# Expert stage of a two-block transformer: the down product of one expert moved behind gate and up of the next

## The chip, the cores and the metric

One core of a Trainium2 chip runs the whole program in one launch. The metric is device time in microseconds (us); lower is better. TensorE does the matmuls, VectorE, ScalarE and GpSimd the elementwise work, SyncE issues the weight loads.

## The reference, cut to what matters

Two transformer blocks over 256 tokens of width 1024. The first block and the attention of the second are dense and are not touched here. The last stage is a mixture of 32 experts, four for each token, followed by a residual sum and a layer norm:

```python
h = xb @ w_gu[e] + b_gu[e]                      # [tokens, 2048], w_gu[e] is [1024, 2048]
h_gate, h_up = jnp.split(h, 2, axis=-1)
h_gate = jnp.minimum(h_gate, 7.0)
h_up = jnp.clip(h_up, -7.0, 7.0)
act = h_gate * jax.nn.sigmoid(1.702 * h_gate) * (h_up + 1.0)
y = act @ w_down[e] + b_down[e]                 # w_down[e] is [1024, 1024]
# out = layer_norm(alpha * h + sum over a token's four experts of gate * y)
```

All weights are float32: 8 MB and 4 MB for each expert, 403 MB (384 units of 1 MB) for the stage.

## The kernel before, in words

Dense layers come first and end in `land` (residual sum, router, each token's slot in its experts). `moe_body` then goes through the 32 experts in turn, each with 64 token slots.

**Weights.** A unit is 1 MB, [128, 2048] float32. An expert has 8 units of `w_gu` (one for each 128 rows, `gate_up`) and 4 of `w_dn` (`down`). `expert_units` sets their order. `fetch` puts each into the next of 21 buffers in turn (pools early, more, xt, merge, ring, parts, moe), by SyncE's queue; a buffer is loaded again when the matmuls that read its old unit are done. `prefetch` fills buffers during the dense layers.

**Half-array work.** With 64 tokens a matmul of `gate_up` (L1260) or `down` (L1292) takes 64 of the array's 128 columns. Two of them, for the two output halves, stand next to each other and run at the same time. A float32 matmul is two instructions, so a unit is 8.

**Whole-array work.** `turn_act` (4 transposes of the activation, L1278), the bias (2 matmuls in `gated_unit`, L1266), `gather` (picks the tokens of two experts by one-hot matmuls, 32 instructions, L1150), `back` (gated one-hots turned, L1204), and `combine` (adds an expert's result into four PSUM sums, 64 rows by 128 columns, 8 instructions, L1375). One-hots and gates of two experts (EG = 2) are made together.

**Order.** For expert e: units 2 to 7 of gate and up; `combine(e - 1)` after the first of these; the bias, then the activation (`gated_unit`, on VectorE and ScalarE); the start of expert e + 1 (its gather, when a new pair begins) and its first unit; `turn_act` of e; the second unit of e + 1 (LEAD = 2); then `down` of e. The scheduler of the language places TensorE's instructions by its own priorities within the dependences, except in the last expert, where the written order holds. The residual is added in two lumps at experts 16 and 31.

```python
u = self.gated_unit(*bank[e])
if e % EG == 0:
    weights(e)
start(e + 1)
product(e + 1, 0)
aT = self.turn_act(u)
for k in range(1, LEAD):
    product(e + 1, k)
y = self.down(aT, lambda i: self.unit_of_expert())
```

`scratch` has 7 buffers for activations, one-hots, results and pick rows; `ps_tr` and `ps_mm` have two PSUM banks each. `rest` is a loop over blocks of tokens beyond an expert's 64 slots.

Of the kernel before, what the change touches and what calls it, by code (L numbers as in the profile page):

```python
# [31 lines left out]
LEAD = 2  # L32
# [20 lines left out]
class Net:  # L53
# [109 lines left out]
    def half_product(self, ps, xT, w, half, js=range(4)):  # L163
        """ps += chunks js of a half of xT times a [4 k, 512] weight unit."""
# [45 lines left out]
    def parts_of(self, ps, hi, lo, gain):  # L210
        """psum chunks [P, n, m] (times gain[:, chunk]) as two float32r parts."""
# [11 lines left out]
    def transposed(self, src, hi, lo, gain=None):  # L223
        """src [P, D] -> its transposed chunks in hi, lo [P, KD, P]."""
# [11 lines left out]
    def begin(self, gu):  # L236
        """The first group's weights and both tiles of x, in BEGIN's order."""
# [29 lines left out]
    def enter(self, t, gain):  # L267
        """x of tile t, turned, with the norm's gain; and its 1 / rms (None without a norm)."""
# [8 lines left out]
    def ffn_body(self, ins, gu, dn, then, hooks):  # L277
        """What enters next: its first tile, and what finishes the second, for when the next first product is out."""
# [75 lines left out]
    def head_norm(self, raw, heads, dh, eps=1e-6, pool=False):  # L354
        """raw [P, heads, dh] normalised over dh in place."""
# [10 lines left out]
    def turn_heads(self, raw, n, outs):  # L366
        """raw [P, n * 128] -> n transposes; outs: (first, count, dest [P, count, P], scale)."""
# [7 lines left out]
    def scores(self, qT, kT, nk, dh):  # L375
        """4 heads' scores [P, 2, 256] x 2: head 2p+s at [s][:, p]."""
# [11 lines left out]
    def softmax(self, sc, nk, bias, scale=True):  # L388
        """exp(score + bias - max) [P, 4, nk], over its row sums unless not scale, and the sums [P, 4]."""
# [27 lines left out]
    def turn_blocks(self, blocks, dest, vector):  # L417
        """Transposes of [P, P] blocks (up to 4) into dest [P, n, P]."""
# [12 lines left out]
    def turn_causal(self, e, t, heads, pT):  # L431
        """e [P, heads, nk] of token tile t into pT [P keys, heads, 3, P]: (tile, key block) 00, 10, 11."""
# [3 lines left out]
    def weigh(self, pT, v, dh, o_hi, o_lo):  # L436
        """Heads' outputs over both token tiles, turned: [P, chunks, T] in two parts; v(h, b): [P, dh]."""
# [23 lines left out]
    def mem_kv(self, l):  # L461
        """Keys (turned) and values of the memory, for layer l."""
# [14 lines left out]
    def rope(self, raw, t):  # L477
        """raw [P, 8, 64]: 4 heads of q, 4 of k -> rotated with the gains."""
# [511 lines left out]
    def route(self, t, ps, less, r):  # L990
        """Which experts tile t's tokens go to, and their slots there (less AWAY); a step a turn."""
# [33 lines left out]
    def gate(self, t):  # L1025
        """Tile t's gates [P, NE], 0 where an expert is not chosen."""
# [13 lines left out]
    def plan_rest(self):  # L1040
        """Blocks of SLOTS tokens beyond an expert's first: how many [1, 1], first and end block per expert."""
# [24 lines left out]
    def rest(self, n, first, end, pick, spare, acc, ln):  # L1066
        """Adds to acc what tokens past an expert's first SLOTS get, one block a turn, by way of two spare tiles,
        and makes the output anew."""
# [3 lines left out]
        with self.tc.For_i(0, n, 1):  # L1072
# [38 lines left out]
            banks = self.gate_up_banks(pk)  # L1111
            for k in range(KD):
                self.gate_up(banks[0], xg[:, k], load(k, gu[0, k * P:(k + 1) * P]), k)
            y = self.down(self.turn_act(self.gated_unit(*banks)),
                          lambda i: load(i, dn[0, i * 256:(i + 1) * 256].rearrange("(c p) d -> p c d", c=2)))
            for h in range(2):
                hs = slice(64 * h, 64 * h + 64)
                for t in range(NT):
# [3 lines left out]
                    nc.tensor.matmul(acc[t][h], gT[t][hs, 0], y[hs], start=False, stop=True)  # L1122
# [21 lines left out]
    def gather_banks(self):  # L1144
        """Where the first gather goes, a bank for two chunks."""
# [6 lines left out]
    def gathered(self, k2, ps, xg):  # L1152
        """Two chunks of what was gathered, with the norm's gain and bias."""
# [9 lines left out]
    def gather(self, hot, xg):  # L1163
        """xg [P, KD, n] = the chosen tokens' columns of x."""
# [8 lines left out]
    def one_hot(self, t, es):  # L1173
        """Tile t's one-hots [P, experts * SLOTS] of the slots of some experts."""
# [11 lines left out]
    def gated(self, hot, gate, n):  # L1186
        """One-hots times gates, twice over: [P, n, 2, SLOTS] per tile."""
# [9 lines left out]
    def back(self, gated, n):  # L1197
        """Gated one-hots turned: per tile [P = (copy, slot), n, P tokens]."""
        nc = self.nc
        out = []  # L1200
        for t in range(NT):
            ps = self.t(self.ps_tr, [P, 4, P], F32, "tr")
            for e in range(n):
                nc.tensor.transpose(ps[:, e], gated[t][:, e].rearrange("p c s -> p (c s)"), self.ident)  # L1204
            gT = self.t(self.moep, [P, n, P], F32, f"back{t}") if n > 1 else self.scr(P).unsqueeze(1)
            nc.scalar.activation(gT, ps[:, :n], AF.Copy, scale=1.0 / 1.702)
            out.append(gT)
        return out

    def expert_units(self):  # L1210
        """The experts' weights in the order of their use: LEAD units of the next one's go before an expert's w_dn."""
        a = self.a
        gu = lambda e, ks: (a["w_gu"][e, k * P:(k + 1) * P] for k in ks)
        yield from gu(0, range(LEAD))
        for e in range(NE):
            yield from gu(e, range(LEAD, KD))
            if e + 1 < NE:
                yield from gu(e + 1, range(LEAD))
            for i in range(4):
                yield a["w_dn"][e, i * 256:(i + 1) * 256].rearrange("(c p) d -> p c d", c=2)  # L1220

    def fetch(self, src=None):
        """The next tile of the rings in turn, with src in it (the last unit in halves)."""
# [15 lines left out]
    def prefetch(self, name, n=None):  # L1239
        """A ring of its own for the experts' first units, loaded ahead (n of them)."""  # L1240
# [7 lines left out]
    def gate_up_banks(self, pick):  # L1248
        nc = self.nc
        ps = [self.t(self.ps_mm, [P, 512], F32, "mm") for _ in range(2)]  # L1250
        pk = self.t(self.scratch, [P, 512], F32R, "s")[:, :2 * SLOTS].rearrange("p (h s) -> p h s", h=2)
        nc.gpsimd.tensor_copy(pk, pick.unsqueeze(2).to_broadcast([P, 2, SLOTS]))
        return ps, pk.rearrange("p h s -> p (h s)")

    def gate_up(self, ps, xk, w, k):
        """ps: the gate's and the up's bank [(half, slot), 512] += x's chunk k . w."""
        for gu in range(2):
            for h in range(2):
                c = gu * D + h * 512
                self.nc.tensor.matmul(ps[gu][64 * h:64 * h + 64], xk, w[:, c:c + 512], start=k == 0, stop=False)  # L1260

    def gated_unit(self, ps, pk):
        """The expert's bias and activation, times 1.702: [(half, slot), 512]."""
        nc = self.nc
        for gu in range(2):
            nc.tensor.matmul(ps[gu], pk, self.brow[:, gu], start=False, stop=True)  # L1266
# [16 lines left out]
    def down(self, aT, unit):  # L1283
        """y [(half, slot), 512]; unit(i): the weights."""
# [18 lines left out]
    def down_bias(self, acc):  # L1303
        """The experts' output biases, times the gates."""
# [12 lines left out]
    def moe_body(self):  # L1317
        nc, a = self.nc, self.a
        hot, banks = self.land()
        acc = [[None, None], [None, None]]  # L1320
        group, bank, back = {}, {}, {}

        def start(e):
            bank[e] = self.gate_up_banks(self.pick[:, e])
            if e % EG == 0:
                es = slice(e, e + EG)
                xg = self.t(self.moep, [P, KD, EG * SLOTS], F32, "xg")
                group[e // EG] = xg, [self.one_hot(t, es) for t in range(NT)] if e else hot
                if e:
                    self.gather(group[e // EG][1], xg)  # L1330

        def product(e, k):
            xg, hot = group[e // EG]
            if e == 0 and k % 2 == 0:
                for j in range(2):
                    for t in range(0 if k >= GATHERED else 1, NT):
                        self.gather_tile(t, k + j, hot[t], banks[k // 2][:, j], t == j == 0, t == j == 1)
                self.gathered(k // 2, banks[k // 2], xg)
            j = e % EG
            self.gate_up(bank[e][0], xg[:, k, j * SLOTS:(j + 1) * SLOTS], self.unit_of_expert(), k)  # L1340

        def weights(e):
            if e == 0:
                for t in range(NT):
                    self.gate(t)
# [209 lines left out]
```

## Time and profile before

| what | value |
|---|---|
| three timed runs | 2157.06, 2160.55, 2159.61 us; median 2159.61 |
| span of the profiled execution | 2158.0 us (no other time is shown for it) |
| TensorE busy (matmul) | 2053.7 us, 95% |
| VectorE, ScalarE, GpSimd busy | 885.3, 691.3, 116.7 us |
| SyncE's weight queue | 596.68 MB |
| mean granted clock of TensorE | 0.988 |

The span runs from the first to the last instruction. Busy time of TensorE is modelled from instructions that overlap in its pipeline, so how much work it does is better read from the distance between starts. The expert stage fills the time from about 1150 us to the end.

### The profile page before, as it was taken

The numbers are of one execution on the slowest core, as the hardware profiler recorded it, in microseconds if no ns is written. First come the engines' busy times: TensorE is split into PE (matmuls) and PEld (weight loads), VectorE is DVE, ScalarE is ACT, GpSimd is POOL, SyncE is SP. The second block draws the span as 40 slices with busy tenths as digits, with TensorE's granted clock in tenths as the row PEclk, the third lists the DMA queues.
The fourth block names the chain that finished last, engine by engine and source line by source line (L and its number), as shares of the span: only waits on it lengthen the run. The fifth ranks groups of instructions, "written<-read, shape, count | busy, mean of one in ns | idle before, by whom it ended". The sixth has DMA issues, their size and how long they took to land.

```text
span 2158.0 us, 24764 instructions
## 1 busy us (share of the span) xinstructions
PE 2053.7 (95%) x9375; PEld 1254.2 (58%) x9375; DVE 885.3 (41%) x2128; ACT 691.3 (32%) x1542; POOL 116.7 (5%) x180
## 2 busy tenths in 40 slices
PE   8999999999999879999999999999999999999996
PEld 7888778888888767888885333333333333333332
DVE  7554876557765887554543110111011011111113
ACT  7454665446553556543541000000000000000000
POOL 0000320000000340000100000000000000000000
PEclk9999999999999999999999999999999999999998
DMA  8463446554554334644569999999999999999980
GB/s 313 175 224 142 144 146 215 190 197 182 193 185 156 139 117 182 228 177 165 202 223 382 364 420 421 421 420 420 417 412 373 389 409 409 420 406 411 408 338 21
DMA packets 101996, 601.98 MB, mean 279 GB/s; under 512 B 10065, under 2 KB 10113, under 8 KB 46193
## 3 DMA queue, kind: packets, MB, share of 16 engines
q1 hardware_dynamic: 100496, 596.68, 70.7%
q0 software_dynamic: 1232, 3.65, 0.5%
q8 instruction: 75, 1.23, 0.2%
q14 instruction: 49, 0.39, 0.0%
q10 hardware_dynamic: 144, 0.03, 0.0%
HBM read 599.27 MB, written 1.05 MB: 278 GB/s over the span
## 4 chain that ended last, share of the span: by engine, by line
PE 89%; DVE 7%; issue 2%; POOL 1%; ACT 1%; DMA 1%; SPq 0%; DVEq 0%; ACTq 0%; POOLq 0%
PE mm L1260 23%; PE tr L1292 10%; PE mm L159 10%; PE mm L160 10%; PE mm L161 10%; PE acc L159 4%; PE acc L1375 4%; PE acc L160 4%; PE acc L161 4%; PE tr L1150 3%; DVE s L1268 1%; PE tr L294 1%; DVE s L1296 1%; PE tr L1278 1%; DVE lo L144 1%
## 5 line engine op out<-in xcount | busy, mean ns | idle before, releaser
L144 DVE TENSOR_TENSOR lo<-w,hi 128x512 fp32r<-128x512 f32 x706 | 455.8, 696 | 189.8 <-ACT hi L142 188.2
L142 ACT ACTIVATE hi<-w 128x512 fp32r<-128x512 f32 x720 | 398.1, 626 | 219.0 <-PE mm L161 92.3
L159 PE MATMUL mm<-hi,w 128*128 128x512 f32 x960 | 383.8, 400 | 3.1 <-ACT w L251 2.7
L160 PE MATMUL mm<-lo,w 128*128 128x512 f32 x960 | 377.5, 394 | 0.6 <-DVE lo L144 0.6
L161 PE MATMUL mm<-hi,w 128*128 128x512 f32 x960 | 376.9, 393 | 0.0
L1260 PE MATMUL mm<-w,xg 128*64 128x512 f32 x1480 | 369.9, 600 | 7.0 <-DVE s L1268 7.0
L1269 ACT ACTIVATE s<-s 128x512 f32<-128x512 f32 x32 | 20.1, 629 | 742.4 <-DVE s L1268 720.7
L1260 PEld LDWEIGHTS mm<-w,xg 128*64 128x64 f32 x1480 | 103.4, 137 | 210.5 <-issue 171.9
L159 PEld LDWEIGHTS mm<-hi,w 128*128 128x128 f32 x960 | 181.7, 189 | 41.7 <-ACT w L251 3.1
L160 PEld LDWEIGHTS mm<-lo,w 128*128 128x128 f32 x960 | 182.0, 190 | 38.0 <-DVE lo L144 2.3
L161 PEld LDWEIGHTS mm<-hi,w 128*128 128x128 f32 x960 | 181.7, 189 | 38.5 <-DVE w L220 0.2
L1268 DVE TENSOR_SCALAR s<-mm 128x512 f32<-128x512 f32 x32 | 22.1, 692 | 413.6 <-PE mm L1266 413.4
L1292 PE MATMUL tr<-w,s 128*64 128x512 f32 x728 | 162.8, 592 | 0.7 <-ACT s L1280 0.7
L1296 DVE COPY s<-tr 128x512 f32<-128x512 f32 x32 | 22.1, 691 | 343.3 <-PE tr L1292 343.3
L159 PE MATMUL acc<-hi,ah 128*128 128x512 f32 x336 | 131.7, 392 | 0.0
L160 PE MATMUL acc<-lo,ah 128*128 128x512 f32 x336 | 130.9, 390 | 0.0
L161 PE MATMUL acc<-hi,al 128*128 128x512 f32 x336 | 130.9, 390 | 0.0
L1375 PE MATMUL acc<-s,back 64*128 64x512 f32 x256 | 92.6, 626 | 22.3 <-DVE s L1296 22.3
L1292 PEld LDWEIGHTS tr<-w,s 128*64 128x64 f32 x728 | 52.6, 137 | 104.1 <-issue 97.4
L1150 PE MATMUL tr<-s,x 128*128 128x128 f32 x496 | 69.5, 289 | 22.1 <-DVE s L1181 21.6
L287 ACT ACTIVATE s<-mm,rs 128x256 f32<-128x256 f32 x88 | 41.7, 474 | 148.2 <-PE mm L161 144.7
L1150 PEld LDWEIGHTS tr<-s,x 128*128 128x128 f32 x496 | 60.8, 196 | 44.5 <-issue 26.7
(328 smaller groups left out, 1976.0 us busy)
## 6 DMA issues: line engine op xcount, KB each, us to landing
w<-w_gu SPq DMA_DIRECT2D x185, 1024.0 KB, 9.7
w<-w_dn SPq DMA_DIRECT2D x90, 1024.0 KB, 9.9
w<-gu SPq DMA_DIRECT2D x86, 1024.0 KB, 4.8
w<-dn SPq DMA_DIRECT2D x44, 1024.0 KB, 4.8
lo<-w_gu SPq DMA_DIRECT2D x36, 1024.0 KB, 10.0
hi<-w_gu SPq DMA_DIRECT2D x35, 1024.0 KB, 9.6
w<-w_in SPq DMA_DIRECT2D x32, 1024.0 KB, 4.8
hi<-w_dn SPq DMA_DIRECT2D x19, 1024.0 KB, 9.5
```

The source lines that it names most:

```text
L142: self.nc.scalar.activation(hi[:, s], raw[:, s], AF.Copy)
L144: engine.tensor_tensor(lo[:, s], raw[:, s], hi[:, s].bitcast(F32), op=ALU.subtract)
L159: mm(out, lh, rh, start=start, stop=False)
L160: mm(out, lh, rl, start=False, stop=False)
L161: mm(out, ll, rh, start=False, stop=stop)
L287: nc.scalar.activation(si, ps[:, :FG], AF.Silu, scale=rs)
L1150: self.nc.tensor.matmul(out, self.x[t][:, k * P:(k + 1) * P], hot, start=start, stop=stop)
L1260: self.nc.tensor.matmul(ps[gu][64 * h:64 * h + 64], xk, w[:, c:c + 512], start=k == 0, stop=False)
L1268: nc.vector.tensor_scalar_min(g, ps[0], 7.0)
L1292: nc.tensor.matmul(py[64 * d:64 * d + 64], aT[:, j, 64 * h:64 * h + 64], w[:, c * D + d * 512:c * D + d * 512 + 512], start=i == 0 and c = ...
L1296: nc.vector.tensor_copy(y, py)
L1375: nc.tensor.matmul(acc[t][h], gT[t][hs, e % EG], y[hs], start=e == 0, stop=e == NE - 1)
```

## The change

TensorE's order is now the written one for the whole stage. A block per expert, `between(e)`, holds all whole-array work: the activation of e - 1 turned, the bias of e (now first in its sums, so it opens the accumulation), the gather of a new pair, `combine(e - 2)`, the turned gates. Then follows one stretch of half-array work: the 8 units of gate and up of e, and the 4 units of down of e - 1. The weights are fetched in that order. One-hots, gated one-hots and pick rows are made one block ahead, on VectorE and GpSimd (`ahead`). The residual comes in pieces in blocks 8 to 13, the output biases in block 3 (before: expert 1). The last norm's rows are fetched before the last four units. `back` turns the gates of both token tiles into one PSUM bank with one copy. The activation of e is computed while down of e - 1 runs.

```diff
-        yield from gu(0, range(LEAD))
-        for e in range(NE):
-            yield from gu(e, range(LEAD, KD))
-            if e + 1 < NE:
-                yield from gu(e + 1, range(LEAD))
-            for i in range(4):
-                yield a["w_dn"][e, i * 256:(i + 1) * 256].rearrange("(c p) d -> p c d", c=2)
+        for e in range(NE + 1):
+            if e < NE:
+                yield from (a["w_gu"][e, k * P:(k + 1) * P] for k in range(KD))
+            if e:
+                yield from (a["w_dn"][e - 1, i * 256:(i + 1) * 256].rearrange("(c p) d -> p c d", c=2)
+                            for i in range(4))
...
+    def gate_up_banks(self, pk):
+
         ps = [self.t(self.ps_mm, [P, 512], F32, "mm") for _ in range(2)]
+        for gu in range(2):
+            self.nc.tensor.matmul(ps[gu], pk, self.brow[:, gu], start=True, stop=False)
+        return ps
...
+        ps = self.t(self.ps_tr, [P, 4, P], F32, "tr")
         for t in range(NT):
-            ps = self.t(self.ps_tr, [P, 4, P], F32, "tr")
             for e in range(n):
-                nc.tensor.transpose(ps[:, e], gated[t][:, e].rearrange("p c s -> p (c s)"), self.ident)
...
+                nc.tensor.transpose(ps[:, t * n + e], gated[t][:, e].rearrange("p c s -> p (c s)"), self.ident)
...
+    def picker(self, pick):
+
+        pk = self.t(self.scratch, [P, 512], F32R, "s")[:, :2 * SLOTS].rearrange("p (h s) -> p h s", h=2)
+        self.nc.gpsimd.tensor_copy(pk, pick.unsqueeze(2).to_broadcast([P, 2, SLOTS]))
+        return pk.rearrange("p h s -> p (h s)")
...
+        def first_gather(k2):
+            for j in range(2):
+                k = 2 * k2 + j
+                for t in range(0 if k >= GATHERED else 1, NT):
+                    self.gather_tile(t, k, hots[0][t], banks[k2][:, j], t == j == 0, t == j == 1)
+            self.gathered(k2, banks[k2], xg[0])
...
+        sums = {8 + 3 * t: residual(t) for t in range(NT)}
+
+        def between(e):
+
+            g = e // EG
+            if e:
+                aT = self.turn_act(u.pop(e - 1))
+            if e < NE:
+                u[e] = self.gate_up_banks(pk.pop(e))
+                if e % EG == 0:
+                    xg[g] = self.t(self.moep, [P, KD, EG * SLOTS], F32, "xg")
+                    if e:
+                        self.gather(hots[g], xg[g])
             if e == 2:
+                plan.append(self.plan_rest())
+            if e >= 2:
+                combine(e - 2)
+            if e % EG == 1:
+                back[g] = self.back(gated.pop(g), EG)
+            if e == 3:
+                self.down_bias(acc)
+            for first, steps in sums.items():
+                if first <= e <= first + 2:
+                    next(steps, None)
+            return aT if e else None
+
+        def ahead(e):
+
+            if e == 0:
+                for t in range(NT):
+                    self.gate(t)
+            if e + 1 < NE:
+                pk[e + 1] = self.picker(self.pick[:, e + 1])
+            g = e // EG
             if e % EG == 0:
+                es = slice(e, e + EG)
+                gated[g] = self.gated(hots[g], [z[:, es] for z in self.gates], EG)
+            elif g < last:
+                es = slice(e + 1, e + 1 + EG)
+                hots[g + 1] = [self.one_hot(t, es) for t in range(NT)]
...
         with self.tc.manual_schedule(engines={mybir.EngineType.PE}):
+            for e in range(NE + 1):
+                aT = between(e)
+                if e < NE:
+                    ahead(e)
+                    for k in range(KD):
+                        if e == 0 and k % 2 == 0:
+                            first_gather(k // 2)
+                        j = e % EG
+                        self.gate_up(u[e], xg[e // EG][:, k, j * SLOTS:(j + 1) * SLOTS], self.unit_of_expert(), k)
+                    u[e] = self.gated_unit(u[e])
+                if e:
+                    y[e - 1] = self.down(aT, lambda i: self.unit_of_expert())
+                if e == 5:
+                    plan = plan[0]
+                    plan[0] = nc.values_load(plan[0][:1, :1], min_val=0, max_val=T * 4 // SLOTS)
+                if e == NE - 1:
+                    ln = self.fetch(a["ln2"])
+            spare = [self.fetch() for _ in range(2)]
+            combine(NE - 1)
```

## Rows read from the trace of the kernel before

**Rows 1.** The page, slices: busy tenths of TensorE, its granted clock, GB/s moved.
```profile
PE   8999999999999879999999999999999999999996
...
PEclk9999999999999999999999999999999999999998
...
GB/s 313 175 224 142 144 146 215 190 197 182 193 185 156 139 117 182 228 177 165 202 223 382 364 420 421 421 420 420 417 412 373 389 409 409 420 406 411 408 338 21
```
**Rows 2.** Waits of SyncE's queue, 1100 to 2158 us: total us, times, longest.
```profile
SPq L1236 <- PE mm L1260: 623.1, 239, 14.2
```
**Rows 3.** Windows, two experts each: us, busy of each engine, clock, DMA share, GB/s.
```profile
1446.55:1508.12 61.57, 57.89 (x258) 21.02 (x257) 8.05 (x18) 4.94 (x10) 0.59 (x2) 1.00 1.02 421
...
1266.05:1323.42 57.37, 55.36 (x257) 20.75 (x257) 8.05 (x18) 5.05 (x10) 0.59 (x2) 1.00 1.02 420
```
**Rows 4.** Chain that ended last, expert stage: start us, us, engine, line, count.
```profile
1280.92 1.92 PE acc L1375 x8
...
1446.55 1.98 PE tr L1150 x16
1448.53 1.86 PE mm L1260 x6
1450.39 0.59 PE tr L1278 x4
...
1452.85 6.89 PE tr L1292 x32
...
1463.57 1.91 PE acc L1375 x6
1465.48 8.73 PE mm L1260 x40
1474.21 0.44 PE mm L1266
```
**Rows 5.** Timeline of TensorE, two experts: start us, us; in brackets the wait before.
```profile
1454.40 1.89 PE L1292 MATMUL tr<-lo,s 128*64 128x512 f32 x8
1456.11 1.89 PE L1292 MATMUL tr<-hi,s 128*64 128x512 f32 x8
...
1460.58 1.12 PE L1375 MATMUL acc<-s,back 64*128 64x512 f32 x2 [0.86 <-DVE s L1296]
...
1504.81 2.32 PE L1150 MATMUL tr<-s,x 128*128 128x128 f32 x16 [1.44 <-DVE s L1181]
```
**Rows 6.** DMA view, 1235 to 1560 us: total; issues, KB, us to landing.
```profile
DMA packets 24109, 136.52 MB, mean 420 GB/s; under 512 B 2082, under 2 KB 2082, under 8 KB 12830
...
w<-w_gu SPq DMA_DIRECT2D x60, 1024.0 KB, 12.7
```
**Rows 7.** DMA view, 1160 to 2110 us.
```profile
DMA packets 68202, 381.13 MB, mean 401 GB/s; under 512 B 5856, under 2 KB 5856, under 8 KB 37568
...
q1 hardware_dynamic: 68096, 380.39, 98.1%
...
s<-b_dn POOLq DMA_DIRECT2D x2, 64.0 KB, 5.7
```
**Rows 8.** Timeline of VectorE, expert 0: first and last of the activation.
```profile
1168.96 0.69 DVE L1268 TENSOR_SCALAR s<-mm 128x512 f32<-128x512 f32 x1 [7.03 <-PE mm L1266]
...
1171.69 0.69 DVE L1271 SCALAR_TENSOR_TENSOR s<-s,s 128x512 f32<-128x512 f32 x1 [0.63 <-ACT s L1269]
```
**Rows 9.** Timeline of TensorE: first units of expert 0.
```profile
1152.72 7.45 PE L1260 MATMUL mm<-w,xg 128*64 128x512 f32 x32
```
**Rows 10.** Windows of 10 us at the stage's start.
```profile
1150.00:1160.00 10.00, 9.98 (x44) 4.47 (x42) 1.05 (x4) 0.91 (x2) 0.00 (x0) 0.83 0.68 249
...
1190.00:1200.00 10.00, 10.00 (x37) 3.02 (x37) 0.00 (x0) 0.00 (x0) 0.00 (x0) 0.83 0.94 356
```
**Rows 11.** Timeline, last weight unit: when its two halves are issued.
```profile
2086.04 0.82 SPq L1234 DMA_DIRECT2D w<-w_dn  x2
```
**Rows 12.** Timeline of TensorE: last down product.
```profile
2132.26 7.09 PE L1292 MATMUL tr<-w,s 128*64 128x512 f32 x32 [0.75 <-ACT s L1280]
```

More of the change, by code (lines that the diff above doesn't have):

```diff
@@ L31 @@
 NE = 32
-LEAD = 2
 EG = 2
@@ L1109, in load @@
                 return spare[i % 2]
-            banks = self.gate_up_banks(pk)
+            banks = self.gate_up_banks(self.picker(pk))
             for k in range(KD):
-                self.gate_up(banks[0], xg[:, k], load(k, gu[0, k * P:(k + 1) * P]), k)
-            y = self.down(self.turn_act(self.gated_unit(*banks)),
+                self.gate_up(banks, xg[:, k], load(k, gu[0, k * P:(k + 1) * P]), k)
+            y = self.down(self.turn_act(self.gated_unit(banks)),
                           lambda i: load(i, dn[0, i * 256:(i + 1) * 256].rearrange("(c p) d -> p c d", c=2)))
@@ L1121, in rest @@
                     nc.tensor.matmul(acc[t][h], self.ident, so_far, start=True, stop=False)
-                    nc.tensor.matmul(acc[t][h], gT[t][hs, 0], y[hs], start=False, stop=True)
+                    nc.tensor.matmul(acc[t][h], gT[hs, t, 0], y[hs], start=False, stop=True)
             self.finish(acc, ln)
@@ L1259, in gate_up, with gated_unit @@
                 c = gu * D + h * 512
-                self.nc.tensor.matmul(ps[gu][64 * h:64 * h + 64], xk, w[:, c:c + 512], start=k == 0, stop=False)
-    def gated_unit(self, ps, pk):
+                self.nc.tensor.matmul(ps[gu][64 * h:64 * h + 64], xk, w[:, c:c + 512], start=False, stop=k == KD - 1)
+    def gated_unit(self, ps):
         nc = self.nc
-        for gu in range(2):
-            nc.tensor.matmul(ps[gu], pk, self.brow[:, gu], start=False, stop=True)
         g, u = self.scr(), self.scr()
@@ L1320, in moe_body @@
         acc = [[None, None], [None, None]]
[L1321 to L1345, printed above, removed]
-            es = slice(e, e + EG)
-            back[e // EG] = self.back(self.gated(group[e // EG][1], [g[:, es] for g in self.gates], EG), EG)
+        xg, hots, gated, back, pk, u, y = {}, {0: hot}, {}, {}, {}, {}, {}
+        last = NE // EG - 1
+        def first_gather(k2):
[4 more added lines that the diff above has]
+            self.gathered(k2, banks[k2], xg[0])
         def residual(t):
-            tiles = []
             for h in range(2):
@@ L1359, in residual, with combine @@
                     nc.vector.tensor_scalar(xT[:, j], ps[:, j], g, b, op0=ALU.mult, op1=ALU.add)
-                tiles.append(xT)
-            return tiles
-        def add_residual(t, tiles):
-            for h in range(2):
+                yield
                 for j in range(4):
-                    nc.tensor.matmul(acc[t][h][:, j * P:(j + 1) * P], tiles[h][:, j], self.ident, start=False, stop=False)
-        def combine(e, y):
+                    nc.tensor.matmul(acc[t][h][:, j * P:(j + 1) * P], xT[:, j], self.ident, start=False, stop=False)
+        def combine(e):
             gT = back[e // EG]
@@ L1374, in combine @@
                         acc[t][h] = self.t(self.ps_acc, [P, 512], F32, f"acc{t}{h}")
-                    nc.tensor.matmul(acc[t][h], gT[t][hs, e % EG], y[hs], start=e == 0, stop=e == NE - 1)
-        start(0)
-        for k in range(LEAD):
-            product(0, k)
-        for e in range(NE):
-            for k in range(LEAD, KD):
-                product(e, k)
-                if e and k == LEAD:
-                    combine(e - 1, y)
-                    if e == 1:
-                        self.down_bias(acc)
-                    if e == NE // 2:
-                        add_residual(0, residual(0))
-                    if e == NE - 1:
-                        last = residual(1)
-            if e == 2:
-                plan = self.plan_rest()
-            if e == 5:
-                plan[0] = nc.values_load(plan[0][:1, :1], min_val=0, max_val=T * 4 // SLOTS)
-            if e == NE - 1:
-                break
-            u = self.gated_unit(*bank[e])
-            if e % EG == 0:
-                weights(e)
-            start(e + 1)
-            product(e + 1, 0)
-            aT = self.turn_act(u)
-            for k in range(1, LEAD):
-                product(e + 1, k)
-            y = self.down(aT, lambda i: self.unit_of_expert())
@@ L1406, in moe_body @@
-        with self.tc.manual_schedule(engines={mybir.EngineType.PE}):
-            u = self.gated_unit(*bank[e])
-            add_residual(1, last)
-            y = self.down(self.turn_act(u), lambda i: self.unit_of_expert())
-        spare = [self.fetch() for _ in range(2)]
-        ln = self.fetch(a["ln2"])
-        combine(NE - 1, y)
+                    nc.tensor.matmul(acc[t][h], gT[hs, t, e % EG], y[e][hs], start=e == 0, stop=e == NE - 1)
+        sums = {8 + 3 * t: residual(t) for t in range(NT)}
@@ new lines, in moe_body @@
+        plan = []
+        pk[0] = self.picker(self.pick[:, 0])
+        with self.tc.manual_schedule(engines={mybir.EngineType.PE}):
+            for e in range(NE + 1):
[17 more added lines that the diff above has]
+            combine(NE - 1)
```

14 lines of the change are left out of this document (3 added, 11 removed).

## The prediction

> **What bounds the kernel now.** I read the page's slices first, then the weight queue, then TensorE. In the slices [rows 1] the run has two halves. Up to the middle the matmul engine is full and the DMA engines move 115 to 315 GB/s: dense layers, bound by TensorE. The change touches nothing there. From about 1150 us the experts run: DMA jumps to about 420 GB/s while TensorE still shows 90%. So two resources are almost equally full, and the question is which of them sets the pace.
>
> The waits of SyncE, which issues the weight loads, answer it: 623 us of standing still at the line that fetches a unit, released by gate and up matmuls that give a buffer back [rows 2]. The 21 buffers are full and the queue waits for TensorE. The pace fits: from expert 6 on two experts take 61.57 us on TensorE; in the first part of the stage it was 57.37 [rows 3]. The first is slower than the queue, the second faster (below). Where TensorE sets the pace the queue falls to 373 to 411 GB/s in many slices; where it doesn't, it holds about 420 [rows 1]. So TensorE binds, by a few per cent, and the queue is the next limit close behind. Both must be priced.
>
> Where do the 61.57 us go? A weight unit (8 matmul instructions on half the array's columns, two at a time) starts 1.71 us after the one before [rows 5]; 32 of them take 6.89 [rows 4]. 24 units are 41.3 us. The rest is 20.3 us, of which pure whole-array work is about 11. What lies between is visible in the chain [rows 4]: gate-up units are cut open by gathers and transposes, and the combine is cut in two. A piece of 6 costs 1.86 where a whole 8 costs 1.72, because its halves no longer run in pairs; the combine in pieces costs 1.12 + 1.91 against 1.92 whole. Each change between half-array and whole-array work costs 0.15 (40 instructions take 8.73, five units are 8.58). And there are waits for VectorE: 0.86 us before the combine, 1.44 before the gather [rows 5].
>
> **The change, part by part: TensorE.** The new order for two experts, summed from the same rows:
> 24 units at 1.72: 41.3. Two entries into the stretch at 0.15: 0.3. Activation transposes, 4 each, twice 0.59: 1.2. Biases, twice 0.44: 0.9. Gather, 16 + 16 at 1.98: 4.0. Combine, twice 1.92: 3.8. Transposed gates, 4: 0.6. Sum 52.1 [rows 4, 5].
> To this I add 0.4: four gather tiles now follow each other through two PSUM banks with no unit between to cover the copy. 52.5 us per pair, 26.3 per expert, against 61.57.
>
> The waits: the activation chain (VectorE clamp to last multiply) took 3.42 us at expert 0, with a table load in it [rows 8]. It now runs under the 6.9 us of the down product before it, so it costs nothing in steady state; expert 0 has no down product before it, so there I count 3.6 once. The copy of a down result (0.86 wait) now runs beside transposes and bias, 0.59 + 0.44 plus an entry: 1.2, so it is covered by 0.3 only; if it were not, 0.3 to 0.9 per expert. The gather's one-hots are made a block earlier (1.44 gone). Bias first instead of last, one larger transposed-gates copy instead of two, and pick rows made a block ahead leave the same or less work, off TensorE. The block for surplus tokens does not run here (no instruction of it is in the trace): nothing.
>
> **The change: the queue.** It fetches the same units, reordered: 8 of an expert, then 4 of the one before. Unhindered it moved 136.52 MB in 325 us: 420 GB/s [rows 6]. A unit of 1.0486 MB takes 2.50 us, 12 take 30.0, a pair 59.9. That is 1.7 us below the 61.57 TensorE takes now, and 7.4 above the 52.5 it will take. So the queue becomes the bound, and most of the 9 us per pair can't be collected. The stage must be summed by the queue.
>
> The Trainium skill's HBM Reference (Specifications) gives about 358 GB/s as a core's effective share and about 425 for a core that streams alone. By 358 the queue would already be the bound and the change would gain nothing (381.13 MB would take 1065 us); by 425, 897 us. The trace agrees with the second: 420 for 325 us.
>
> **The sum.** From 1160 us to its end the queue moved 381.13 MB [rows 7]. At 420 GB/s that is 907.5 us: if it never stands still, the last weight lands at 2067.5. Now it is issued at 2086 [rows 11]: the queue loses some 26 us to full buffers.
> Will it still stand still? Only if 21 units more have landed than TensorE has used. At 1160 the equivalent of 22.2 have landed (385 units with the last norm's rows, less 380.39 / 1.0486, the part of the 381.13 MB that is SyncE's queue [rows 7]). Expert 0 starts around 1150 to 1152 [rows 9] and, with its gather pieces in front of each two units, ends near 1170; with the 3.6 us the next stretch starts at about 1175: 28 landed, limit 29. The third stretch starts near 1203: 39.4, limit 41. Block 3 holds the output biases too: their load lands 5.7 us after issue [rows 7] and is asked for only when scratch is free, so TensorE waits up to 6 us, then 8 matmuls and transposes, 9 in all. Stretch at 1237: 53 landed, limit 53. I take 2.5 us lost here; bounds 0 (bias load early) and 8 (15 us instead of 9, and a second stop). In the kernel before, the queue lost about 4 and 2 us in two 10 us slices of its start (249 and 356 GB/s against 420 [rows 10]).
> After that TensorE uses 12 units in 26.3 us and gets 12 in 30.0: the reserve of about 20 units (50 us) shrinks 3.7 us per expert and is gone near expert 17. The residual pieces, now spread over six blocks, and the register load fall into that reserve: nothing. From there TensorE waits for each unit.
> Last weight: 2067.5 + 2.5 = 2070. Before, the last unit of the last down product began at 2132.26 + 3 x 1.72 = 2137.4 [rows 12], 20.6 us before the end of the span at 2158.0; copy, combine and final norm behind it do not change. The halved load of the last unit now falls on another unit, and the norm's rows are fetched ahead of the last four; the first is in the full 1.72, the second in the bytes. New span: 2070 + 0.4 for the wait on the landing + 20.6 = 2091.
> So 2158.0 - 2091 = 67 us, in two parts: 39 us that TensorE trailed the queue (buffers full to the end), 26 to 28 us of queue standstill. No other time is shown for the profiled execution; its span lies 1.6 below the median of the three runs, 2159.61. I put the 67 against the median: 2093 us.
>
> **The rivals.**
> A (the sum): queue bound, 2085 to 2103. Low end: no standstill, 422 GB/s as in its best slices, first buffer freed 2 us sooner. High end: 8 us standstill and a few at the tail. Chance 0.74.
> B: the queue is slower with 20 loads outstanding than with the 5 it had (landing 12.7 us after issue, five times 2.5 [rows 6]); or the 373 to 411 of the later slices was not the buffers' doing. With 402 GB/s over the later half, 450 us cost 20 more: 2112. For it: nothing shown ran that deep. Against: the 623 us of waits for buffers [rows 2]. Chance 0.10.
> C: TensorE stays the bound, because written order exposes waits: of 0.86 and 1.44 as now, or VectorE's own order holding up the activation. Needed is 3.7 us per block before it costs anything; stepping through the blocks, 3 us more in each ends at a span of 2117 (the reserve is never restored and TensorE trails again), 4 us at 2149, 4.3 us at no change. Against: the waits now, 0.86 twice and 1.44 once in two experts, are some 1.6 us per expert [rows 5]. Chance 0.10, of which 0.02 within 0.2% and 0.01 slower.
> D, the slower one: the clock. From expert 17 on TensorE waits for weights in every block. It fell to 0.83 in 10 us at 1190, after the small output-bias matmuls, so dips are at hand [rows 10]. At the lower level (1.2 GHz) a unit takes 3.43. If the first half of each stretch ran so, a block grows by 10.3 to 36.6 us, 6.6 above the queue's 30.0; 15 blocks: 99 us, so 2192. It turns the gain into a loss from about 5 units of each block at the low level (8.1 us). Against: with 0.86 and 1.44 us stops in each pair the clock stayed at 1.00 through the stage [rows 1, 3], a TensorE at half clock uses up its waits by working longer, and no slice of the run fell below 0.9 [rows 1] but the last. Chance 0.06.
> The Trainium skill's page TensorE: Matmul & The Clock Gate, in its section on HAM oscillation, tells of a matmul kernel that waits for weights in every step and finds its clock low each time: D is that rule. No stage here shows it, since TensorE has hardly waited for DMA.
>
> **How the numbers follow.** Likeliest A: 2093. About 0.2% is what a measurement of this kernel can tell from no change. Faster: A, B, and 0.07 of C, 0.91; same 0.02; slower 0.07 (0.01 of C and D). To leave out no more than 2 in 10 the range takes A and B and the lower edge of C: 2083 to 2120; it holds about 0.85.
>
> **What will show it.** Right: the weight queue near 420 GB/s in every slice from 1240 to its end near 2070; SyncE's waits for matmuls small; TensorE's idle time from the second half of the experts released by DMA of weights, about 3 to 4 us per expert; blocks of 26 to 28 us before that; chain with 96 instructions in one piece per expert and no x2 and x6 pieces; the final norm some 20 us after the last landing. Wrong: clock below 1.00 in the second half (D), DMA share below 1 with TensorE waiting for it (B), TensorE idle on VectorE or ScalarE in each block (C).

## The result, and the profile after

The changed kernel takes 2099.78 us (median of four runs, 2098.64 to 2101.37), the kernel before 2158.86: a ratio of 0.973, interval 0.9718 to 0.9741, so 59 us faster. The forecast was 2093 us, 67 us less. The profiled run took 2101.37 us, its span is 2099.7, against 2158.0 before.

The page's slices of after: busy tenths of TensorE, granted clock, GB/s, to be held against [rows 1].

```profile
PE   8999999999999988999999999999999998889995
...
PEclk9999999999999998999999989999999999999998
...
GB/s 321 181 211 151 141 154 216 186 188 153 214 185 199 140 81 189 230 183 191 162 168 320 374 382 419 421 421 420 419 421 421 420 420 421 420 420 420 421 420 245
```

From the 25th slice to the last but one the weight queue holds 419 to 421 GB/s. The 373 to 411 of the later slices of before [rows 1] are gone. Two things are not as forecast: slices 23 and 24 (374 and 382), the start of the stage, and the last (245). Most of the drop in the last slice is the tail, in which no weight moves; a queue at 420 GB/s up to 2079.7 us, where the last weight is used, would still show some 280 there.

Waits of after. First those of SyncE from 1100 to 2100 us (its engine and line, what it waited for, total us, times, longest), which answer to [rows 2]; then those of TensorE on weights from 1630 to 2082 us, the last fifteen blocks.

```profile
SPq L1231 <- PE mm L1261: 228.2, 121, 17.9
SPq L1231 <- DMA w<-w_gu: 164.1, 100, 2.9
SPq L1231 <- DMA w<-w_dn: 138.6, 70, 2.2
...
PE tr L1291 <- DMA w<-w_dn: 20.2, 38, 1.5
PE mm L1261 <- DMA w<-w_gu: 9.2, 18, 0.6
...
PE tr L1291 <- DMA hi<-w_dn: 3.6, 6, 0.6
PE tr L1291 <- DMA lo<-w_dn: 3.5, 6, 0.6
PE mm L1261 <- DMA lo<-w_gu: 2.1, 4, 0.6
PE mm L1261 <- DMA hi<-w_gu: 1.7, 3, 0.6
```

SyncE waited 623.1 us for matmuls before [rows 2], now 228.2. That is less, but not the small amount that the forecast gave as a sign; 123.0 of it come after 1290 us, where the queue holds 420 GB/s all the same, so a wait of SyncE is not by itself a standstill of the queue. The second and third rows are new: SyncE waits some 2 us at a time for an earlier load to land. That is no loss either, since the transfers keep running behind it. TensorE, which hardly waited for weights before, now waits 40.3 us in these fifteen blocks (the six rows summed). The two have changed places, as the forecast had it.

The chain that ended last in after, in order of time (start us, us, engine, line, count), against [rows 4]: two experts, the ends of the three pairs with the residual in them, the place where the chain reaches the queue, and the end.

```profile
1263.32 0.59 PE tr L1277 x4
...
1270.24 13.88 PE mm L1261 x64
1284.12 6.87 PE tr L1291 x32
...
1315.31 0.59 PE tr L1277 x4
...
1367.29 0.59 PE tr L1277 x4
...
1541.18 0.59 PE tr L1277 x4
...
1626.09 19.90 DMA w<-w_dn
...
2062.35 17.33 DMA w<-w_dn
2079.72 1.96 PE tr L1291 x8
```

A stretch is one piece of 96 instructions (13.88 + 6.87 us); the x2 and x6 pieces of [rows 4] are gone. From 1263.32 to 1315.31 is one pair: 51.99 us, where before took 61.57 [rows 3]. From 1367.29 to 1541.18, with the residual pieces, three pairs take 173.9 us, 17.9 more than three times 51.99; the queue ran at 415 GB/s or more there, so this cost nothing, as forecast. At 1626 the chain jumps to a weight transfer. And the last unit is used at 2079.72, on the landing of its weight; what is left to the end of the span is 20.0 us.

TensorE's timeline of after (start us, us, line, operation, shapes, count, in brackets the wait before): block 1, block 3, two units of block 17, and the last unit.

```profile
1173.56 1.12 PE L1277 MATMUL tr<-ident,s 128*128 128x128 f32 x4 [2.66 <-DVE s L1270]
...
1231.83 3.75 PE L1314 MATMUL acc<-s,s 32*128 32x512 f32 x4 [2.83 <-DMA s<-b_dn]
...
1643.58 1.94 PE L1291 MATMUL tr<-w,s 128*64 128x512 f32 x8 [0.52 <-DMA w<-w_dn]
1646.03 1.94 PE L1291 MATMUL tr<-w,s 128*64 128x512 f32 x8 [0.51 <-DMA w<-w_dn]
...
2079.72 1.94 PE L1291 MATMUL tr<-w,s 128*64 128x512 f32 x8 [1.46 <-DMA w<-w_dn]
```

The units of block 17 start 2.45 us apart, the queue's pace; in [rows 5] they start 1.71 apart, TensorE's own.

Windows of after (stretch, us, busy of each engine with counts, clock, share of the DMA engines, GB/s), the first two against [rows 10].

```profile
1160.00:1170.00 10.00, 8.99 (x48) 4.04 (x48) 0.82 (x2) 0.92 (x2) 0.30 (x1) 1.00 0.98 351
1170.00:1180.00 10.00, 7.34 (x32) 3.41 (x30) 2.66 (x5) 3.11 (x4) 0.00 (x0) 0.83 0.81 304
1180.00:1190.00 10.00, 10.00 (x50) 3.33 (x48) 0.24 (x1) 0.00 (x0) 0.00 (x0) 1.00 0.98 392
...
1230.00:1240.00 10.00, 7.80 (x11) 2.45 (x11) 0.68 (x3) 0.00 (x0) 0.00 (x0) 0.57 1.01 401
1240.00:1250.00 10.00, 10.00 (x37) 3.14 (x38) 0.00 (x0) 0.00 (x0) 0.00 (x0) 0.75 0.63 244
...
1385.00:1410.00 25.00, 23.48 (x108) 8.95 (x106) 4.80 (x10) 1.82 (x3) 0.29 (x1) 0.93 1.02 422
...
1985.00:2010.00 25.00, 20.38 (x91) 5.73 (x88) 2.56 (x4) 0.63 (x1) 0.30 (x1) 1.00 1.02 418
...
2070.00:2080.00 10.00, 7.87 (x34) 2.43 (x36) 0.00 (x0) 0.44 (x1) 0.00 (x0) 1.00 0.55 226
```

The DMA view of after, 1160 to 2082 us, against [rows 7]:

```profile
DMA packets 68165, 380.57 MB, mean 413 GB/s; under 512 B 5856, under 2 KB 5856, under 8 KB 37632
```

The five windows up to 1250 us fall 69, 116, 28, 19 and 176 GB/s short of 420: 408 x 10 us / 420 = 9.7 us of standstill. In the last window the queue runs out: 226 GB/s over 9.7 us is 4.3 to 4.6 us less than full speed. Together: 1160 + 380.57 MB / 420 GB/s (906.1) + 9.7 + 4.3 = 2080.1, and the last weight is used at 2079.72. The span from 1160 us on is thus accounted for: a queue at 420 GB/s, two losses of its own, and a tail of 20.0.

### The profile page after: what moved, and what is told of

Same layout as the page of the kernel before. It is cut to its first block, busy times and chain, and to the rows that moved or that the text cites. A ratio compares the mean times of both kernels' runs of the same rounds, so it can differ in the third digit from the quotient of the medians.

```text
span 2099.7 us, 24826 instructions
## 1 busy us (share of the span) xinstructions
PE 1989.6 (95%) x9375; PEld 1240.6 (59%) x9375; DVE 894.0 (43%) x2128; ACT 690.5 (33%) x1526; POOL 117.0 (6%) x180
## 4 chain that ended last, share of the span: by engine, by line
PE 75%; DMA 16%; DVE 5%; issue 2%; ACT 1%; POOL 1%; SPq 0%; DVEq 0%; POOLq 0%; ACTq 0%
PE mm L1261 14%; DMA w<-w_dn 10%; PE mm L158 10%; PE mm L159 10%; PE mm L160 10%; PE tr L1291 7%; PE acc L158 4%; PE acc L159 4%; PE acc L160 4%; PE acc L1353 3%; PE tr L1149 2%; DMA lo<-w_dn 2%; DMA hi<-w_dn 2%; PE tr L293 1%; DVE lo L143 1%
## 5 line engine op out<-in xcount | busy, mean ns | idle before, releaser
L1261 PE MATMUL mm<-w,xg 128*64 128x512 f32 x1464 | 330.8, 603 | 11.2 <-DMA w<-w_gu 9.2
L1291 PE MATMUL tr<-w,s 128*64 128x512 f32 x744 | 172.1, 598 | 22.9 <-DMA w<-w_dn 20.2
L1279 ACT ACTIVATE s<-tr 128x512 f32<-128x512 f32 x32 | 19.1, 598 | 257.4 <-PE tr L1277 257.4
L287 DVE SCALAR_TENSOR_TENSOR s<-mm,rs,s 128x256 f32<-128x256 f32 x88 | 42.4, 482 | 107.2 <-ACT s L286 105.0
L1261 PE MATMUL mm<-hi,xg 128*64 128x512 f32 x296 | 71.0, 600 | 1.7 <-DMA hi<-w_gu 1.7
## 6 DMA issues: line engine op xcount, KB each, us to landing
w<-w_gu SPq DMA_DIRECT2D x183, 1024.0 KB, 19.6
```

The lines of the kernel that those rows point to most:

```text
L287: nc.vector.scalar_tensor_tensor(av, ps[:, FG:], rs, si, op0=ALU.mult, op1=ALU.mult)
L1291: nc.tensor.matmul(py[64 * d:64 * d + 64], aT[:, j, 64 * h:64 * h + 64], w[:, c * D + d * 512:c * D + d * 512 + 512], start=i == 0 and c = ...
```

## The experiments

**Does the queue set the pace now, and did TensorE before?** In each, one half of every fourth down unit isn't loaded, and its matmuls use the loaded half twice: 16.8 MB less, the same instructions on TensorE. The changed kernel's list of loads is shown, shortened; the kernel before got the same in 31 of its 32 experts (16.3 MB).

```diff
-  for i in range(4): ... w_dn[e - 1, i * 256:(i + 1) * 256] ...
+  for i in range(4): ... w_dn[e - 1, i * 256:(i + 1) * 256] ... [:, :2 if i < 3 else 1]
```

> Of every fourth down unit only the first half is loaded, and its matmuls use that half twice (the result is not the reference's); TensorE's instructions are as many as before. 16.8 MB less for the queue. If the weight queue paces the changed kernel from the middle of the experts on: stepping block by block through landings and uses gives a span some 36 us shorter, about 2064 us (2058 to 2070). If TensorE still paces it: no change, 2100.

> The same cut of bytes in the kernel before (31 of 32 experts; the result is not the reference's). If TensorE paced that kernel, as its buffer waits say: at most 3 us gained, 2156 to 2160. If the queue already paced it: about 39 us gained, 2120.

Changed kernel: 2063.74 us, ratio to before 0.9563 (0.9547 to 0.9579), 36 less than with all bytes (16.8 MB take 40 us at 420 GB/s). Kernel before: 2157.59, ratio 1.0002 (0.9992 to 1.0012). A window of each, first of the changed kernel, then of before:

```profile
1885.00:1935.00 50.00, 45.81 (x224) 17.31 (x220) 6.48 (x15) 4.25 (x8) 0.59 (x2) 1.00 1.01 421
```

```profile
1446.55:1508.12 61.57, 57.89 (x259) 21.01 (x257) 8.06 (x18) 4.94 (x10) 0.59 (x2) 1.00 0.96 392
```

With fewer bytes the changed kernel's queue still runs at 421 GB/s, TensorE still has idle time (45.81 of 50 us busy), and the time falls with the bytes. In the kernel before two experts take 61.57 us with 392 GB/s as with 421 [rows 3]; the bytes are worth nothing. So the bound has moved from TensorE to the queue.

**How much room is there on TensorE?** The gather's matmuls are done two and three times over into the same sums.

```diff
-                for t in range(NT):
+                for t in list(range(NT)) * N:     # N = 2, 3
```

> The changed kernel with every gather matmul of pairs 1 to 15 done twice into the same sums: 4.0 us more TensorE work for each pair, 59 us in all. If the queue paces, most of it falls into TensorE's waits for weights: stepping through the blocks gives 6 us more, about 2106 (2102 to 2112). If TensorE paces: 59 more, 2159.

> Three times: 8 us more per pair, 118 in all. The slack of about 3.6 us per expert is used up and TensorE takes over: stepping gives 49 us more, about 2149 (2142 to 2156). If TensorE paced all along: 118 more, 2218. If the queue had far more room than thought: under 2115.

Twice: 2103.42 us, ratio 0.975 (0.9733 to 0.9766). Three times: 2136.82, ratio 0.9904 (0.9888 to 0.9921). The second was expected at 2149, at least 2142. Its chain:

```profile
1611.82 0.59 PE tr L1277 x4
...
1637.18 10.73 PE tr L1149 x96
...
1670.58 0.59 PE tr L1277 x4
```

From 1611.82 to 1670.58 a pair takes 58.76 us, 6.8 more than the 51.99 of the changed kernel: a repetition costs 3.4 us, not the 4.0 I had counted. With 96 instructions in a row one takes 10.73 / 96 = 0.112 us, so 32 take 3.6; the rest of the 4.0 is the wait for copies that a single round has. That is why the forecast of 2149 was too high. The pair's 58.76 is below the queue's 59.9, and yet the run is 37 us slower than the changed kernel. The reason is the reserve of the start, some 20 units or 50 us of weights already landed: with 0.6 us gained per expert, some 16 in 28 blocks, most of it is left to the end, and in this run TensorE waits for no weight. The loss shows in two places, first in a window with the residual pieces, then in TensorE's last down product:

```profile
1485.00:1535.00 50.00, 46.97 (x260) 24.49 (x260) 9.58 (x23) 4.25 (x8) 0.59 (x2) 0.97 0.92 375
...
2108.94 7.09 PE L1291 MATMUL tr<-w,s 128*64 128x512 f32 x32
```

The buffers are full, so the queue stands still wherever TensorE is slow (375 GB/s here, 339 from 1235 to 1285 us): the last weight, issued at 2081.24 and 16.9 us on its way, lands near 2098, some 18 us later than in the changed kernel. And its unit begins at 2114.1 (2108.94 + 3 x 1.72), 16 us after it has landed. Together that is the 34 us between the spans, 2134.1 and 2099.7.

**What held the start and the end up?** Three moves in the changed kernel, each alone, then together: the output biases in block 6 instead of 3; the gather pieces of the first expert all ahead of its units; the last norm's rows fetched after the last weights.

```diff
-            if e == 3:
+            if e == 6:
                 self.down_bias(acc)
...
-                        if e == 0 and k % 2 == 0:
-                            first_gather(k // 2)
+                        if e == 0 and k == 0:
+                            for k2 in range(KD // 2):
+                                first_gather(k2)
...
-                if e == NE - 1:
-                    ln = self.fetch(a["ln2"])
+            ln = self.fetch(a["ln2"])
             spare = [self.fetch() for _ in range(2)]
```

> The changed kernel with the output biases in block 6 instead of block 3. If the 4 us that the queue stands still near 1245 come from full buffers while TensorE waits for the bias load and runs its small matmuls at the low clock: by block 6 the reserve has shrunk, the queue does not stop, 4 to 6 us gained, about 2095. If the stop has another cause, or the time is lost to TensorE and not to the queue: no change, 2100.

> The changed kernel with the four first-gather pieces of expert 0 all ahead of its eight units, not one in front of each two. Three waits of 0.5 us and six changes of array mode go; expert 0 ends some 3 us sooner, so the queue stands still that much less near 1175: 2 to 3 us gained, about 2097. If the first units' later release costs as much: no change, 2100.

> The changed kernel with the last norm's rows fetched behind the last weights, as in the kernel before. If the queue sets the end, 1 MB less stands ahead of the last weight: 2.5 us gained, about 2097; the norm's rows land 2.5 us behind it, before they are needed. If the slow landing of the last units (the queue moves 233 GB/s in its last 10 us) is what sets the end, the drain takes the gain: 0 to 1 us.

> All three together. If they are three separate stops of the queue, the gains add: 9 to 12 us, about 2089 (2087 to 2092). If they are not the queue's, 2097 to 2100.

| kernel | median us | ratio to before (interval) |
|---|---|---|
| changed | 2099.78 | 0.973 (0.9718 to 0.9741) |
| biases in block 6 | 2096.28 | 0.9716 (0.9702 to 0.9729) |
| first gather ahead | 2095.25 | 0.9708 (0.9694 to 0.9721) |
| norm's rows last | 2097.79 | 0.9723 (0.9709 to 0.9736) |
| all three | 2091.00 | 0.9691 (0.9677 to 0.9704) |

Each alone is at the edge of what the measurement resolves (its interval overlaps that of the changed kernel); all three are clearly faster, by 8.8 us, and the singles sum to 10.0. Where the bytes come back can be read in the windows. Biases in block 6:

```profile
1230.00:1240.00 10.00, 10.00 (x50) 3.43 (x48) 0.00 (x0) 0.00 (x0) 0.00 (x0) 1.00 1.01 426
1240.00:1250.00 10.00, 10.00 (x49) 3.19 (x46) 2.11 (x4) 0.63 (x1) 0.00 (x0) 1.00 1.03 412
```

First gather ahead:

```profile
1160.00:1170.00 10.00, 8.87 (x42) 2.73 (x38) 1.38 (x2) 1.18 (x1) 0.00 (x0) 1.00 1.00 419
1170.00:1180.00 10.00, 8.47 (x38) 4.09 (x40) 1.27 (x3) 1.93 (x4) 0.00 (x0) 0.83 1.00 406
```

Part of this is only moved: from 1150 to 1160 us the rate is now 214 GB/s, where the changed kernel has 293. Over these windows up to 1190 us the queue gains 2.5 us net; the profiled spans differ by 2.7 (2097.0 and 2099.7), the medians by 4.5.

Norm's rows last, TensorE's timeline: the last down product is unbroken, where in the changed kernel its last unit waited 1.46 us. The queue ends as slowly as before, but now it is the norm's rows that come last, and TensorE doesn't wait for them.

```profile
2070.17 7.09 PE L1291 MATMUL tr<-w,s 128*64 128x512 f32 x32
```

All three, the DMA view from 1160 to 2085 us in 40 slices: no standstill is left, only the end.

```profile
GB/s 418 419 423 417 421 422 413 423 414 423 420 422 418 420 423 419 423 413 424 420 423 418 418 425 417 424 414 424 420 422 419 419 425 418 423 416 423 421 417 142
```

**Is it the block, or the written order?** The kernel before with its own sequence and weights, but TensorE's instructions in written order; the changed kernel with the scheduler's order; and that with the three moves.

```diff
 kernel before
+        with self.tc.manual_schedule(engines={mybir.EngineType.PE}):   # around the loop over experts
 changed kernel
-        with self.tc.manual_schedule(engines={mybir.EngineType.PE}):
+        if True:
             for e in range(NE + 1):
```

> One part of the change alone: the kernel before with TensorE held to the written order through the whole expert loop, weights and blocks as they were (down of e not moved behind gate and up of e + 1). If the cut pieces and waits came from the scheduler's placing: combine whole, gathers whole, about 56 to 57 us per pair by TensorE, which is below the queue's 59.9: the queue paces and the time is near that of the whole change, 2100 to 2112. If the one block per expert is what is needed: the written order exposes the activation chain and the one-hot waits, 60 us or more per pair, 2140 or more.

> The other part alone: the changed kernel without the written order; the scheduler places TensorE's instructions within the dependences. If moving the work into one block is enough, TensorE stays below the queue's pace: 2098 to 2106. If the scheduler cuts the pieces open again, as it did: toward 57 to 61 us per pair, 2110 to 2150.

> All three moves of the run before (biases in block 6, first gather ahead, norm's rows last) without the written order. The scheduler's order already had the first gather ahead and hid most of expert 0's activation under the next units, and it waited 1.4 us instead of 2.8 for the bias load; so of the three only the norm's rows (2 us) and a little of the bias are still to be had: 2089 to 2092, the same as with the written order. If its order carried a gain of its own of 4.5 us, it adds: 2086 to 2088.

Written order alone: 2133.71 us, ratio 0.9892 (0.9876 to 0.9909). Block alone: 2095.29, ratio 0.9712 (0.9696 to 0.9729). Block with the three moves in the scheduler's order: 2091.33, ratio 0.9689 (0.9676 to 0.9702), the same as in written order (2091.00). The first lies between the two expectations. Its timeline of TensorE:

```profile
1446.69 3.98 PE L1150 MATMUL tr<-s,x 128*128 128x128 f32 x30 [0.25 <-DVE s L1181]
...
1477.18 0.81 PE L1204 MATMUL tr<-ident,s 128*128 128x128 f32 x4 [2.29 <-DVE s L1192]
...
1504.36 3.98 PE L1150 MATMUL tr<-s,x 128*128 128x128 f32 x30 [0.25 <-DVE s L1181]
```

and its DMA view from 1160 to 2130 us, 40 slices of 24.25 us:

```profile
GB/s 363 344 339 421 400 408 416 424 418 423 417 421 421 421 421 418 420 419 426 415 424 415 423 420 422 418 422 420 421 422 417 423 416 426 418 423 417 391 11 45
```

A pair takes 57.67 us, 3.9 less than before: the units are whole, but TensorE waits 2.29 us for the gated one-hots. That is enough for the queue to run at some 420 GB/s after the first six slices and to be done by about 2083 us, 3 us after that of the changed kernel. But the span ends at 2129.7, some 46 us later: TensorE still has the reserve to work off, and in the last expert a lump of the residual (some 6 us) and the activation stand in its way too; the last 20 are the tail. The block alone in the scheduler's order takes 55.94 us for a pair (chain):

```profile
1555.45 13.91 PE mm L1261 x64
...
1611.39 13.88 PE mm L1261 x63
```

That is 4 us more than in written order and costs nothing, since the queue is the bound.

## Why the forecast was right, and where its size was off

**TensorE's pair: right.** 52.5 us were summed; the chain shows 51.99.

**The queue becomes the bound at 420 GB/s: right (rival A).** 420 GB/s in the slices, time falling with the bytes, TensorE's waits on weights in place of SyncE's on matmuls. The reserve was to be gone near expert 17; the chain reaches the queue in block 17, at 1626 us. That the block came out right is in part luck: the residual pieces slowed TensorE by 17.9 us and made the reserve last longer, the losses at the start made it smaller. TensorE's waits were forecast at 3 to 4 us per expert; the waits view shows 40.3 / 15 = 2.7. The rest is how busy time is modelled: a unit that ends alone shows 1.94 us where units in a row start 1.72 apart, 0.22 for each of 75 waits, 1.1 us per expert more.

**The gain of 67 in two parts.** 59 came, and the split into 39 and 26 to 28 was wrong. The time from issue to landing of the last weight's two halves in the kernel before (DMA view, 1160 to 2110 us) shows it:

```profile
w<-w_dn SPq DMA_DIRECT2D x2, 512.0 KB, 6.9
```

Issued at 2086.04 [rows 11], the last weight landed near 2093, 44 us before its unit began (2137.4): 44 us were trailing, and the forecast of 2070 for the last weight held 23 us for the queue. The 44 came whole: the last unit now begins as its weight lands. The tail behind it is 20.0 where 20.6 + 0.4 were counted. The queue's part is the one that came short: the last weight lands at 2079.7, 14 us sooner instead of 23.

**The step that was mis-sized: 2.5 us of standstill at the start.** It measured 9.7, above its upper bound of 8. I had looked for it in block 3 alone. There TensorE waits 2.83 us for the bias load, under the 6 I allowed, but the windows with the 32-row matmuls and the first units behind them show 0.57 and 0.75 of the clock, so the buffers come free late: 176 + 19 GB/s short, 4.6 us. As much is lost before that, at expert 0 and block 1 (69 + 116 + 28 GB/s, 5.1 us), where I had taken the queue to run through. TensorE's times there were as forecast: expert 0 ends at 1170.1, the next stretch begins at 1176.3 (1170 and 1175), with the gather pieces before each two units and the wait of 2.66 us for the activation in them. So was the count at 1175: 374.41 MB were still to come, so 385 - 374.41 / 1.0486 = 27.9 units had landed (forecast 28, limit 29). What failed is the test: "only if 21 units more have landed than TensorE has used" lets the queue run at its full rate up to the limit. It was at 351 GB/s from 1160 to 1170 us already, and at the end of that window 26.1 units had landed (376.31 MB to come). A load holds its buffer from its issue on, so the loads on their way have to fit under the limit too. That reading is worked out from these counts; no run tested it alone. With the biases three blocks later 3.5 us come back, with the gather ahead 4.5 by the medians and 2.7 by the profiled spans; the windows place them in these two losses.

**A term that was missing: the end of the queue.** I let the last unit land at the full rate. In fact the last 9.7 us run at 226 GB/s, some 4.3 us lost. Of rival B (a queue slower when deep) no more than this is true: up to there it holds 420. Moving the norm's megabyte behind the last weight, one unit or 2.5 us, gave 2.0 by the medians and 4.4 by the profiled spans (2095.3 and 2099.7). The queue still ends slowly in it, but TensorE's last four units no longer wait for it. In the kernel before, whose last loads landed 5 to 7 us after their issue, the end was sharp: 391 and 344 GB/s in its last two windows of 2 us, some 0.5 us lost.

With 9.7 in place of 2.5, 4.3 added, and the measured bytes and tail, the sum is 1160 + 906.1 + 14.0 + 20.0 = 2100.1 against a span of 2099.7.

**Rival C (TensorE stays the bound): not here, but its condition was right.** The forecast said that some 3 us more per block bring the trailing back well before TensorE's pace meets the queue's. The kernel with three gathers is that case: 3.4 us more per expert, 37 us lost. Sorted by TensorE's time for a pair, 61.57 took 2159 us, 58.76 took 2137, 57.67 took 2134, 55.94 took 2095, 55.2 (two gathers, by its chain) took 2103 and 51.99 took 2100. My estimate from these rows of where it turns: 50 us of reserve over some 28 blocks is 1.8 per expert, so 59.9 - 3.6 = 56.3 for a pair. The three above it are slow by TensorE, which trails the queue and stops it; the three below it lie within 8 us of each other.

**Rival D (the clock): it did not come.** From block 17 on TensorE waits about 0.5 us before many of its units and the clock stays at 1.00, as in the window from 1985 us. It did fall elsewhere, to 0.93 in the window from 1385 us, where the residual's short transposes stand with three waits of 0.51 us between them, but there the reserve covered it. The Trainium skill's page TensorE: Matmul & The Clock Gate, in its section on HAM oscillation, describes a matmul kernel whose clock falls at each wait for the next slice of an operand. Each of its waits is longer than the about 2 us of matmuls that stand before it; here the longest on a weight is 1.5 us, and the trace from block 17 on doesn't show that rule at work.

**The weight rate.** The Trainium skill's HBM Reference (Specifications) gives two figures, and the trace agrees with the one for a core that streams alone: 420 GB/s from 1250 us until the queue runs out, not 358.

What stays open: whether the slow end of the queue comes from how many loads are on their way, and whether another split of the last units would avoid it; neither was tried.

## What to carry to other kernels

Where two resources are within a few per cent of each other, speeding up the binding one gains down to the other, and then every us that the other stands still counts in full: sum the queue's bytes, and look for its standstills at the start and the end of the stage. A reserve that was filled ahead is a debt at the end: as long as the consumer is only slightly faster than the queue, it is still working the reserve off when the last byte has landed, so the whole gain comes only when it is faster by the reserve over the number of steps (here 1.8 us per expert, by the estimate above). Once the other resource binds, a perfect order is no longer needed: here the block alone, with the scheduler's order, did as well.

## What the runs showed of the hardware

**Eight loads in flight.** After the change SyncE waits 164.1 and 138.6 us for earlier loads; on the page a unit of `w_gu` lands 19.6 us after its issue, about eight times 2.5 us. From block 17 on TensorE uses each unit as it lands, so most of the 21 buffers are free then, and SyncE still waits for earlier loads; what sets the eight isn't shown. It cost no bandwidth: the queue holds 420 GB/s.

```profile
w<-w_gu SPq DMA_DIRECT2D x183, 1024.0 KB, 19.6
```

**A queue that runs dry ends slowly.** Windows of 2 us at the end, changed kernel (columns as above):

```profile
2072.00:2074.00 2.00, 1.75 (x10) 0.57 (x8) 0.00 (x0) 0.00 (x0) 0.00 (x0) 1.00 0.68 281
2074.00:2076.00 2.00, 1.60 (x10) 0.55 (x10) 0.00 (x0) 0.00 (x0) 0.00 (x0) 1.00 0.56 231
2076.00:2078.00 2.00, 2.00 (x12) 0.42 (x8) 0.00 (x0) 0.00 (x0) 0.00 (x0) 1.00 0.39 154
2078.00:2080.00 2.00, 0.54 (x4) 0.20 (x4) 0.00 (x0) 0.00 (x0) 0.00 (x0) 1.00 0.13 53
```

From 2072 us the rate falls in steps to 53 GB/s, and with it the mean busy share of the 16 DMA engines, from 0.68 to 0.13.

**The clock.** It fell to 0.57 in the 10 us with the 2.83 us wait and the small output-bias matmuls and to 0.93 in 25 us with the residual's transposes, and held 1.00 through fifteen blocks with a wait before many of the units.
